# Rotated keys in one stacked tile, read once; queries' high and low parts held in both halves

## The chip, the cores and the metric

The kernel runs on one core of one Trainium2 chip. The metric is the device time of one execution in microseconds, lower is better. Of the kernel before there are three timed runs, and one more execution that was taken with a profile.

## What is computed

One layer of a bidirectional encoder for two sequences, a prompt of 512 tokens and a sample of 256, both 2048 wide, with shared weights. The kernel treats them as one block of 768 columns (`T`). Cut to what matters here:

```python
h = rmsnorm(x, ln_mix_g); z = h @ w_in         # [fourier 1024 | q 1024 | k 256 | v 256]
q, k = apply_rope(q, cos, sin), apply_rope(k, cos, sin)
s = einsum('bnqhgd,bnkhd->bnhgqk', qb, kb) * HEAD_DIM ** -0.5   # 16 q heads, 4 kv heads, width 64
p = exp(s - m) / (sum(exp(s - m)) + exp(sink - m))              # window of +-128 positions
mixed = concat([rmsnorm(of), rmsnorm(p @ v)])
x = x + mixed @ w_out
u = relu(rmsnorm(x) @ w_up); x = x + (u * u) @ w_down           # 2048 -> 8192 -> 2048
return rmsnorm(x, ln_final_g)
```

## The kernel before

All matrix products are made at nearly full float32 precision: an operand is split into a high part (rounded to the type that TensorE multiplies, `F32R`) and a low part (what is left), and three products, high by high, high by low and low by high, are added up in PSUM. Scores are an exception with a trick, described below.

**Stages.** The program runs through four stretches on one TensorE queue, whose order is written out by hand:

1. Norm of x, v projection, and the Fourier columns of `w_in` (in the profile up to 173.5 us).
2. Twenty pieces of q and k columns of `w_in` (five pairs of 128-column blocks, four pieces each; the products are `pz`, L802), with the Fourier transform between them, and the rotation of keys and queries beside them on the other engines (173.5 to 379 us).
3. Attention, 24 units (six blocks of 128 queries times four kv heads), interleaved with the first half of the output projection `pm` (L1046; 379 to 589 us). A unit is four heads. The order of this stretch is set by a list of events at due times (`t_qk`, `t_lq` and the like), counted in slots of the output projection.
4. The rest of the output projection, `w_up` (`pu`, L1193) and `w_down` (`pd`, L1628), to the end.

**Rotation and split (`cross`, `turned`, `parts`).** Columns come out of TensorE into PSUM and are copied by ScalarE to a tile `zs` of 128 partitions, two blocks and 768 columns (L815). Pair 0 holds the keys; it and pair 1 are parked in DRAM first and loaded back by `load_z`. GpSimd and VectorE rotate `zs` in place, ScalarE writes the high part to `zh`, VectorE writes the low part over `zs`, and ScalarE's DMA queue puts both into DRAM (L704): `kh`, `kl` for keys, `qh0` to `qh3` and `ql0` to `ql3` for queries. The tile `zs` has one buffer in the pool `kp` and one in the pool `zo`; pairs 0, 1 and 4 use the first in turn, pairs 2 and 3 the second. So pair 3 can be copied out of PSUM only when pair 2 has been put into DRAM.

**Scores (`qk`, L848).** A head is 64 wide, so one unit's query tile `qs` holds the high part in partitions 0 to 63 and the low part in 64 to 127. The keys stand in two tiles of 128 partitions: `kdh` has the high part in both halves, `kdl` the low part in both. Two products per head give (high + low) by low and (high + low) by high:

```python
def load_k(i):                                                        # L717
    h = slice(i % 2 * HD, (i % 2 + 1) * HD)
    nc.sync.dma_start(f32(kt["kdh" if i < 2 else "kdl"][h]), kr_d[i // 2][:].rearrange("(d h) t -> d h t", h=NKV))
...
qs = kt["kp"].tile([P, 4, P], F32R, tag="qs", name="qs", bufs=2)      # L727, in load_q
for o in range(2):
    nc.sync.dma_start(f32(qs[o * HD : (o + 1) * HD]), qr_d[g][o][:, t0].rearrange("(d h) t -> d h t", h=4))
...
for i in range(4):                                                    # L755
    after(14.5 + i, lambda i=i: load_k(i))
```

`load_k` (L719) makes four loads of 768 KB into 64 partitions each. `load_q` (L730) makes two loads of 128 KB per unit, into the two halves of one of two `qs` buffers; unit u + 2 is asked for when unit u's scores are done, since it takes unit u's buffer. Until the first units, the same two buffers serve as `zh`.

**Queues.** SP issues the loads: weights (`raw`, L79 and L162), Fourier outputs (`ofr`, L188), attention outputs (`oar`, L965), keys and queries. ScalarE's queue issues the puts: `kh` to `ql3`, attention outputs `oad` (L940) and projection results `y1` (L1079). Each queue issues in the order of its program, and an issue that waits holds back everything behind it. DMAs of both queues take eight completion semaphores in turn, and an issue also waits until the DMA that had its semaphore before, eight back over both queues, has landed. SP's order is written by a scheduler up to piece 18, and by hand from piece 19 through attention.

Of the kernel before, what the change touches and what calls it, by code (L numbers as in the profile page):

```python
# [11 lines left out]
F32 = mybir.dt.float32  # L12
F32R = mybir.dt.float32r
# [7 lines left out]
P = 128  # L21
# [3 lines left out]
T = SEQ + DSEQ  # L25
# [6 lines left out]
NKV = 4  # L32
HD = 64
# [7 lines left out]
def hybrid_encoder(ctx: ExitStack, tc: tile.TileContext, a: dict):  # L41
    nc = tc.nc
    ctx.enter_context(tc.manual_schedule(engines={mybir.EngineType.PE}))

    def f32(ap):
        return ap.bitcast(F32)
# [3 lines left out]
    dpool = ctx.enter_context(tc.tile_pool(name="dpool", bufs=1, space=DRAM))  # L50
# [63 lines left out]

    zf_d = [dpool.tile([P, T], F32, tag=f"zf{i}", name=f"zf{i}") for i in range(FG)]
    zs_d = [dpool.tile([2 * P, T], F32, tag=f"zs{i}", name=f"zs{i}") for i in range(2)]
    kr_d = [dpool.tile([2 * P, T], F32, tag=f"k{c}", name=f"k{c}") for c in "hl"]
    qr_d = [[dpool.tile([2 * P, T], F32, tag=f"q{c}{i}", name=f"q{c}{i}") for c in "hl"] for i in range(NKV)]
    of_d = dpool.tile([FG * P, T], F32, tag="of", name="ofd")
    oa_d = [dpool.tile([NH * HD, P], F32, tag=f"oa{i}", name=f"oad{i}") for i in range(NM)]  # L120
# [77 lines left out]
    with ExitStack() as ph:  # L198
# [454 lines left out]
        zo = {}  # L653

        kt = {}

        def open_attention():
            kp = kt["kp"] = kctx.enter_context(tc.tile_pool(name="kp", bufs=1, side="right", reuse_waits="tile"))
            for name, shape, src in (
                ("mask", [P, 384], a["c_mask"]), ("cosr", [P, T], a["c_cos"]), ("sinr", [P, T], a["c_sin"]),  # L660
                ("sink", [P, 64], a["attn_sink"].partition_broadcast(P)),
            ):
                kt[name] = kp.tile(shape, F32, tag=name, name=name)
                nc.sync.dma_start(kt[name][:, : src.shape[1]], src)
            for t in (kt["cosr"][:], kt["sinr"][:]):
                nc.vector.tensor_tensor(out=t, in0=t, in1=rb[:], op=ALU.mult)
            for name in ("kdh", "kdl"):
                kt[name] = kp.tile([P, NKV, T], F32R, tag=name, name=name)

        zt = {}  # L670
        t_zl, t_zp = 1.1, 1.9

        def z_tile(pair):
            zt[pair] = (zo["p"] if pair in (2, 3) else kt["kp"]).tile([P, 2, T], F32, tag="zs", name="zs")

        def load_z(pair):
            z_tile(pair)
            nc.sync.dma_start(zt[pair][:], zs_d[pair][:].rearrange("(b p) t -> p b t", p=P))
# [10 lines left out]
        def turned(pair, s):  # L689

            ts = slice(s * 256, (s + 1) * 256)
            z, y = zt[pair][:, :, ts], ys.pop((pair, s))
            cb = kt["cosr"][:, ts].rearrange("p (o t) -> p o t", o=1).to_broadcast([P, 2, 256])
            nc.vector.tensor_tensor(out=z, in0=z, in1=cb, op=ALU.mult)
            for b, op in enumerate((ALU.subtract, ALU.add)):
                nc.vector.tensor_tensor(out=z[:, b], in0=z[:, b], in1=y[:, b], op=op)  # L696

        def parts(pair, s, when=lambda dt, fn: fn()):

            ts = slice(s * 256, (s + 1) * 256)  # L700
            z = zt[pair][:, :, ts]
            out, scale = (kr_d, None) if pair == 0 else (qr_d[order[pair]], HD ** -0.5)
            hi = kt["kp"].tile([P, 2, 256], F32R, tag="zy" if pair == len(cols) - 1 else "qs", name="zh", bufs=2)
            put = lambda o, x: nc.scalar.dma_start(out[o][:, ts].rearrange("(b p) t -> p b t", p=P), x)  # L704
            if scale is None:
                nc.scalar.activation(hi[:], z, AF.Copy)
                low = lambda: nc.vector.tensor_tensor(out=z.bitcast(F32R), in0=z, in1=f32(hi[:]), op=ALU.subtract)
            else:
                nc.scalar.activation(hi[:], z, AF.Copy, scale=scale)
                low = lambda: nc.vector.scalar_tensor_tensor(  # L710
                    out=z.bitcast(F32R), in0=z, scalar=scale, in1=f32(hi[:]), op0=ALU.mult, op1=ALU.subtract
                )
            put(0, f32(hi[:]))
            when(t_zl, low)
            when(t_zp, lambda: put(1, z))

        def load_k(i):  # L717
            h = slice(i % 2 * HD, (i % 2 + 1) * HD)
            nc.sync.dma_start(f32(kt["kdh" if i < 2 else "kdl"][h]), kr_d[i // 2][:].rearrange("(d h) t -> d h t", h=NKV))  # L719

        units = [(b, g) for b in range(NM) for g in range(NKV)]
        state = {}
# [1 line left out]
        def load_q(u):  # L724
            b, g = units[u]
            t0 = slice(b * P, (b + 1) * P)
            qs = kt["kp"].tile([P, 4, P], F32R, tag="qs", name="qs", bufs=2)  # L727
            state[u] = {"qs": qs}
            for o in range(2):
                nc.sync.dma_start(f32(qs[o * HD : (o + 1) * HD]), qr_d[g][o][:, t0].rearrange("(d h) t -> d h t", h=4))  # L730

        todo = {}

        def after(piece, fn):
            todo.setdefault(piece, []).append(fn)

        for g in range(FG):
# [6 lines left out]
            after(p0 + 2, lambda g=g: stage2(g))  # L744
        after(10, fourier_norm)
        after(10, open_attention)
        cols = [2048, 1536, 1024, 1280, 1792]
        order = [None, 2, 0, 1, 3]
        for pair, t, ahead in ((0, 10.5, 10), (2, 11.5, None), (3, 15, None), (1, 16.5, 12)):
            if ahead is not None:  # L750
                after(ahead, lambda pair=pair: load_z(pair))
            for s in range(3):
                after(t + s // 2 * 0.5, lambda pair=pair, s=s: cross(pair, s))
                after(t + 0.5 + s // 2 * 0.5, lambda pair=pair, s=s: (turned(pair, s), parts(pair, s)))
        for i in range(4):  # L755
            after(14.5 + i, lambda i=i: load_k(i))
        for u in range(2):
            after(18 + 0.5 * u, lambda u=u: load_q(u))
        after(18, lambda: load_of(0, [kt["kp"].tile([P, 4, P], F32, tag="zy", name="ofr", bufs=2) for _ in range(2)]))
# [28 lines left out]
        for piece in range(n_in):  # L788
            pair, j = divmod(piece, 4)
# [6 lines left out]
            for c in range(2):  # L796
                cs = slice(c * P, (c + 1) * P)
                for i in range(4):
                    first, stop = j == 0 and i == 0, j == 3 and i == 3
                    for w, o, n in ((wh, 0, 0), (wh, 1, 1), (wl, 0, 2)):  # L800
                        for s in range(2):
                            nc.tensor.matmul(  # L802
                                ps[c][s][:, :HALF], w[:, i, cs], whole[j // 2][s][o][:, 4 * (j % 2) + i, :],
                                start=first and n == 0, stop=stop and n == 2,
                            )
                if j == 3:
                    if c == 0 and pair >= 2:
                        z_tile(pair)
                    if pair < 2:
                        zs = fp.tile([P, T], F32, tag="zs", name="zs", bufs=2)  # L810
# [19 lines left out]
    att = ExitStack()  # L830
    ap_ = att.enter_context(tc.tile_pool(name="att", bufs=2, reuse_waits="tile"))
    pp3 = att.enter_context(tc.tile_pool(name="pp3", bufs=1, space=PSUM, reuse_waits="tile"))
    mask, sink, kdh, kdl = (kt[c] for c in ("mask", "sink", "kdh", "kdl"))

    def key_blocks(b):
        lo, hi = (0, 3) if b < 4 else (4, 5)
        return max(lo, b - 1), min(hi, b + 1)

    def qk(u, heads):
        b, g = units[u]  # L840
        k0, k1 = key_blocks(b)
        nk = (k1 - k0 + 1) * P
        st = state[u]
        for h in heads:
            s = tiles.pop("s", None) or pp3.tile([P, 512], F32, tag="s", name="s", bufs=3)
            st[f"s{h}"] = s
            for n, kd in enumerate((kdl, kdh)):
                nc.tensor.matmul(s[:, :nk], st["qs"][:, h, :], kd[:, g, k0 * P : k0 * P + nk], start=(n == 0), stop=(n == 1))  # L848

    def row_max(u, heads):  # L850
        b, g = units[u]
# [152 lines left out]
    for u in range(len(units)):  # L1004
        t = pace * u + t_first
        for h in range(4):
            dt = t_qk + d_qk * h
            at(t + dt, lambda u=u, h=h: qk(u, (h,)))
            at(t + dt + t_max, lambda u=u, h=h: row_max(u, (h,)))
            at(t + dt + t_exp, lambda u=u, h=h: exps(u, (h,)))  # L1010
        at(t + t_norm, lambda u=u: normalize(u))
        if u + 2 < len(units):
            at(t + t_lq + 2 * (u == 1), lambda u=u: load_q(u + 2))
        for kb in range(3):
            at(t + t_trans + d_trans * kb, lambda u=u, kb=kb: trans(u, kb))
            at(t + t_pv + d_pv * kb, lambda u=u, kb=kb: pv(u, kb))
    for s in range(3):
        at(t_cross[s], lambda s=s: cross(len(cols) - 1, s))
        at(t_turn[s], lambda s=s: turned(len(cols) - 1, s))
        at(t_parts[s], lambda s=s: parts(len(cols) - 1, s, later))  # L1020
# [472 lines left out]
    order = (4, 2, 6, 0, 1, 3, 5)  # L1493
# [62 lines left out]
    def put(m, q, gained, queue=nc.sync):  # L1556
        y = acc4(m, q)
        if gained:
            nc.scalar.activation(y, y, AF.Copy, scale=ry[:, m : m + 1])
        else:  # L1560
            nc.vector.scalar_tensor_tensor(
                out=y, in0=y, scalar=ry[:, m : m + 1], in1=ep["gf"][:, q * 512 : (q + 1) * 512], op0=ALU.mult, op1=ALU.mult
            )
        queue.dma_start(out_rows(m)[:, q * 512 : (q + 1) * 512], y)
# [73 lines left out]
    left_terms = {1: (a21_d, s_d[3])}  # L1638
    HP = NFF // 4
    kept, parts, ep = {}, {}, {}  # L1640

    dunits = [(kh, i, j) for kh in range(2) for i in order for j in range(HP // 2)]
# [169 lines left out]
```

## Time and profile before

| | |
|---|---|
| time, median of 3 runs | 2589.92 us (2589.88 to 2593.62) |
| the profiled execution's own time | 2589.64 us |
| its span in the profile | 2587.8 us |
| granted TensorE clock | 0.999 |
| busy TensorE, VectorE, ScalarE, GpSimd | 100%, 70%, 43%, 10% of the span |
| moved by DMA | 489.55 MB, 189 GB/s on average |

How to read it: a row of the timeline or of a group names engine, line, operation, the tile written and the tiles read. PE is TensorE's matmul, PEld its weight load, DVE is VectorE, ACT is ScalarE, POOL is GpSimd; SPq and ACTq are the DMA queues of SP and ScalarE. "Idle before" is idle time of that engine just ahead of the row, and the name behind the arrow is what ended it. The time to landing of a DMA runs from its issue until its completion semaphore is full.

### The profile page before, as it was taken

The numbers are of one execution on the slowest core, as the hardware profiler recorded it, in microseconds if no ns is written. First come the engines' busy times: TensorE is split into PE (matmuls) and PEld (weight loads), VectorE is DVE, ScalarE is ACT, GpSimd is POOL, SyncE is SP. The second block draws the span as 40 slices with busy tenths as digits, with TensorE's granted clock in tenths as the row PEclk, the third lists the DMA queues.
The fourth block names the chain that finished last, engine by engine and source line by source line (L and its number), as shares of the span: only waits on it lengthen the run. The fifth ranks groups of instructions, "written<-read, shape, count | busy, mean of one in ns | idle before, by whom it ended". The sixth has DMA issues, their size and how long they took to land.

```text
span 2587.8 us, 34953 instructions
## 1 busy us (share of the span) xinstructions
PE 2575.5 (100%) x13580; PEld 2358.4 (91%) x13580; DVE 1812.4 (70%) x2222; ACT 1124.0 (43%) x1574; POOL 249.6 (10%) x353
## 2 busy tenths in 40 slices
PE   9999999999999999999999999999999999999998
PEld 9999998888899999999999999988888888888887
DVE  7966568776555656555877877667776765777687
ACT  6545437674333333333444554433333333333335
POOL 1001332232201011000000000110000000000000
PEclk9999999999999999999999999999999999999999
DMA  7963385345664445456666666775543662555364
GB/s 255 309 223 113 126 237 185 115 138 192 220 197 156 162 161 187 160 189 240 212 213 232 230 215 208 245 304 178 181 155 112 219 234 82 179 179 164 99 207 155
DMA packets 268999, 489.55 MB, mean 189 GB/s; under 512 B 19568, under 2 KB 164000, under 8 KB 267424
## 3 DMA queue, kind: packets, MB, share of 16 engines
q1 hardware_dynamic: 197328, 321.26, 39.0%
q10 hardware_dynamic: 58688, 115.18, 11.8%
q0 software_dynamic: 12816, 50.87, 5.8%
q8 instruction: 107, 1.75, 0.3%
q14 instruction: 60, 0.49, 0.1%
HBM read 360.35 MB, written 126.88 MB: 188 GB/s over the span
## 4 chain that ended last, share of the span: by engine, by line
PE 94%; DVE 2%; DMA 1%; POOL 1%; ACT 0%; issue 0%; SPq 0%; ACTq 0%; POOLq 0%; DVEq 0%
PE pu L1193 36%; PE pd L1628 35%; PE pm L1046 9%; PE p L268 5%; PE pz L802 4%; PE pv L391 1%; PE o L924 1%; PE s L848 1%; PE t L905 1%; POOL zy L687 1%; DMA raw<-in_w_in 1%; PE ptx L137 0%; DVE zs L696 0%; PE pa L609 0%; PE pe L630 0%
## 5 line engine op out<-in xcount | busy, mean ns | idle before, releaser
L1193 PE MATMUL pu<-xf,wh 128*128 128x384 f32 x3072 | 780.8, 335 | 0.0
L1193 PEld LDWEIGHTS pu<-xf,wh 128*128 128x128 f32 x3072 | 554.2, 188 | 1.5 <-ACT o L1211 1.3
L1628 PE MATMUL pd<-wl,sh 128*128 128x512 f32 x1332 | 518.3, 389 | 0.0
L1628 PE MATMUL pd<-wh,sh 128*128 128x512 f32 x1332 | 518.3, 389 | 0.0
L1628 PE MATMUL pd<-wh,sl 128*128 128x512 f32 x1332 | 518.1, 389 | 0.0
L1193 PE MATMUL pu<-xf,wl 128*128 128x384 f32 x1536 | 513.7, 334 | 0.0
L1605 ACT ACTIVATE wh<-rd 128x1024 fp32r<-128x1024 f32 x200 | 202.4, 1054 | 522.2 <-PE pd L1628 416.9
L1615 DVE TENSOR_TENSOR wl<-rd,wh 128x1024 fp32r<-128x1024 f32 x200 | 236.2, 1222 | 226.1 <-ACT wh L1605 225.4
L1173 ACT ACTIVATE wh<-ur 128x1024 fp32r<-128x1024 f32 x160 | 170.0, 1063 | 382.5 <-PE pu L1193 201.8
L1628 PEld LDWEIGHTS pd<-wh,sl 128*128 128x128 f32 x1332 | 250.1, 188 | 52.0 <-DVE sl L1616 0.3
L1628 PEld LDWEIGHTS pd<-wh,sh 128*128 128x128 f32 x1332 | 250.2, 188 | 51.5
L1628 PEld LDWEIGHTS pd<-wl,sh 128*128 128x128 f32 x1332 | 250.2, 188 | 51.5
L1193 PEld LDWEIGHTS pu<-xf,wl 128*128 128x128 f32 x1536 | 288.6, 188 | 0.0
L1179 DVE TENSOR_TENSOR wl<-ur,wh 128x1024 fp32r<-128x1024 f32 x160 | 195.6, 1222 | 76.0 <-ACT wh L1173 76.0
L1214 DVE TENSOR_TENSOR o<-pu,o 128x768 f32<-128x768 f32 x160 | 152.9, 956 | 122.4 <-PE pu L1193 114.8
L1598 DVE TENSOR_TENSOR rd<-rd 128x1024 f32<-128x1024 f32 x112 | 131.8, 1219 | 0.0
L1193 PE MATMUL pu<-xs,wh 128*128 128x384 f32 x512 | 130.0, 334 | 0.0
L1173 ACT ACTIVATE wh<-sx 128x1024 fp32r<-128x1024 f32 x64 | 67.8, 1061 | 130.5 <-PE pu L1193 105.0
L268 PE MATMUL p<-xs,wh 128*128 128x384 f32 x448 | 114.0, 335 | 0.0
L1616 DVE TENSOR_TENSOR sl<-sr,sh 128x768 fp32r<-128x768 f32 x111 | 105.7, 952 | 0.0
L1179 DVE TENSOR_TENSOR wl<-sx,wh 128x1024 fp32r<-128x1024 f32 x64 | 78.2, 1223 | 23.8 <-ACT wh L1173 23.6
L1193 PEld LDWEIGHTS pu<-xs,wh 128*128 128x128 f32 x512 | 92.5, 188 | 0.0
(279 smaller groups left out, 3914.6 us busy)
## 6 DMA issues: line engine op xcount, KB each, us to landing
rd<-in_w_down SPq DMA_DIRECT2D x176, 512.0 KB, 5.2
ur<-in_w_up SPq DMA_DIRECT2D x128, 512.0 KB, 4.0
sr<-sd SPq DMA_DIRECT2D x95, 384.0 KB, 5.4
pd<-o ACTq DMA_DIRECT2D x60, 384.0 KB, 2.3
o<-pd POOLq DMA_DIRECT2D x60, 384.0 KB, 5.9
sd<-sm ACTq DMA_DIRECT2D x60, 384.0 KB, 2.7
raw<-in_w_in SPq DMA_DIRECT2D x38, 512.0 KB, 5.9
raw<-in_w_out SPq DMA_DIRECT2D x32, 512.0 KB, 4.2
```

Of the source, the lines that this page charges most:

```text
L268: nc.tensor.matmul(ps7[bank, g, r][:, :HALF], l[:, i, r * P : (r + 1) * P], x[:, o, 4 * e + i, :], start=(opens and e == 0 and i == 0 and ...
L802: nc.tensor.matmul(ps[c][s][:, :HALF], w[:, i, cs], whole[j // 2][s][o][:, 4 * (j % 2) + i, :], start=first and n == 0, stop=stop and n == 2,)
L1046: nc.tensor.matmul(ps, l(k), w[:, k % 2, :], start=(k == 0 and n == 0), stop=(k == 7 and n == 2))
L1173: nc.scalar.activation(wh[:], raw[:], AF.Copy)
L1179: nc.vector.tensor_tensor(out=wl[:], in0=raw[:], in1=f32(wh[:]), op=ALU.subtract)
L1193: nc.tensor.matmul(ps[:, t, :HALF], w[:, i, t * P : (t + 1) * P], xb[:, o, i, :], start=(s == first_of[bank] and i == 0 and n == 0), stop= ...
L1214: nc.vector.tensor_tensor(out=o, in0=src, in1=o, op=ALU.add)
L1598: add = lambda x, y, op: nc.vector.tensor_tensor(out=x[:], in0=x[:], in1=y[:], op=op)
L1605: nc.scalar.activation(wh[:], t[:], AF.Copy)
L1615: nc.vector.tensor_tensor(out=wl[:], in0=t[:], in1=f32(wh[:]), op=ALU.subtract)
L1616: nc.vector.tensor_tensor(out=sl[:], in0=sr[:], in1=f32(sh[:]), op=ALU.subtract)
L1628: nc.tensor.matmul(o, l[:, q, ts], w[:, ns], start=(j == j0 and (q, t) == (0, 0)), stop=(j == j1 and (q, t) == (1, 2)),)
```

## The change

High and low parts of the keys go to one DRAM tensor of 512 rows and are read by one load of 1536 KB into one tile `kd`: high part in partitions 0 to 63, low part in 64 to 127. Both products of a head now read `kd`; what differs is the query operand, whose tile holds the high part in both halves and the low part in both halves, and is loaded by four DMAs of 128 KB per unit in place of two. A unit's products are now low by (high + low) and high by (high + low), two per head as before and of the same sizes. The space that one key tile of 12 KB per partition leaves goes to the larger `qs` buffers and to a second `zs` buffer in `kp`; `zh` uses half of a `qs` buffer. The load of the keys is asked for once, after piece 15, in place of four times from piece 14.5 on.

```diff
-    kr_d = [dpool.tile([2 * P, T], F32, tag=f"k{c}", name=f"k{c}") for c in "hl"]
+    kr_d = dpool.tile([4 * P, T], F32, tag="k", name="k")
...
-            for name in ("kdh", "kdl"):
-                kt[name] = kp.tile([P, NKV, T], F32R, tag=name, name=name)
+            kt["kd"] = kp.tile([P, NKV, T], F32R, tag="kd", name="kd")
...
-            zt[pair] = (zo["p"] if pair in (2, 3) else kt["kp"]).tile([P, 2, T], F32, tag="zs", name="zs")
+            zt[pair] = zo["p"].tile([P, 2, T], F32, tag="zs", name="zs") if pair in (2, 3) else kt["kp"].tile([P, 2, T], F32, tag="zs", name="zs", bufs=2)
...
-            out, scale = (kr_d, None) if pair == 0 else (qr_d[order[pair]], HD ** -0.5)
-            hi = kt["kp"].tile([P, 2, 256], F32R, tag="zy" if pair == len(cols) - 1 else "qs", name="zh", bufs=2)
+            out, scale = ([kr_d[o * 2 * P : (o + 1) * 2 * P] for o in range(2)], None) if pair == 0 else (qr_d[order[pair]], HD ** -0.5)
+            if pair == len(cols) - 1:
+                hi = kt["kp"].tile([P, 2, 256], F32R, tag="zy", name="zh", bufs=2)
+            else:
+                hi = kt["kp"].tile([P, 2, 4, P], F32R, tag="qs", name="zh", bufs=2)[:, 0].rearrange("p (b h) t -> p b (h t)", b=2)
...
-        def load_k(i):
-            h = slice(i % 2 * HD, (i % 2 + 1) * HD)
-            nc.sync.dma_start(f32(kt["kdh" if i < 2 else "kdl"][h]), kr_d[i // 2][:].rearrange("(d h) t -> d h t", h=NKV))
+        def load_k():
+            nc.sync.dma_start(f32(kt["kd"][:]), kr_d[:].rearrange("(p h) t -> p h t", h=NKV))
...
-            qs = kt["kp"].tile([P, 4, P], F32R, tag="qs", name="qs", bufs=2)
+            qs = kt["kp"].tile([P, 2, 4, P], F32R, tag="qs", name="qs", bufs=2)
             state[u] = {"qs": qs}
-            for o in range(2):
-                nc.sync.dma_start(f32(qs[o * HD : (o + 1) * HD]), qr_d[g][o][:, t0].rearrange("(d h) t -> d h t", h=4))
+            for i in range(2):
+                for o in range(2):
+                    nc.sync.dma_start(f32(qs[i * HD : (i + 1) * HD, o]), qr_d[g][o][:, t0].rearrange("(d h) t -> d h t", h=4))
...
-        for i in range(4):
-            after(14.5 + i, lambda i=i: load_k(i))
+        after(15, load_k)
...
-            for n, kd in enumerate((kdl, kdh)):
-                nc.tensor.matmul(s[:, :nk], st["qs"][:, h, :], kd[:, g, k0 * P : k0 * P + nk], start=(n == 0), stop=(n == 1))
+            for o in range(2):
+                nc.tensor.matmul(s[:, :nk], st["qs"][:, 1 - o, h, :], kd[:, g, k0 * P : k0 * P + nk], start=(o == 0), stop=(o == 1))
```

SP's order around the keys, where `raw` is the next weight piece and `zs<-zs` the load of a parked pair (the number names its DRAM tensor). Before:

```order
L678 DMA zs<-zs_78 128x2x768
L79 DMA raw<-in_w_in 128x4x256 x2
L719 DMA kdh<-kh 64x3072
L678 DMA zs<-zs_79 128x2x768
L79 DMA raw<-in_w_in 128x4x256
L719 DMA kdh<-kh 64x3072
L79 DMA raw<-in_w_in 128x4x256
L719 DMA kdl<-kl 64x3072
L79 DMA raw<-in_w_out 128x2x512
L719 DMA kdl<-kl 64x3072
L79 DMA raw<-in_w_out 128x2x512
```

And now:

```order
L677 DMA zs<-zs_78 128x2x768
L79 DMA raw<-in_w_in 128x4x256
L677 DMA zs<-zs_79 128x2x768
L79 DMA raw<-in_w_in 128x4x256
L720 DMA kd<-k 128x3072
L79 DMA raw<-in_w_in 128x4x256 x2
L79 DMA raw<-in_w_out 128x2x512 x2
```

Three loads are gone from among the weight loads, the parked pair 1 is loaded two places earlier, and the one load of keys stands where the first of the four stood.

SP's order at attention units 3 and 4, where `qh_88` is the high part of head group 3, `qh_82` that of group 0, and `ofr` and `raw` are loads for the output projection. Before:

```order
L730 DMA qs<-qh_88 64x4x128
L730 DMA qs<-ql_89 64x4x128
L188 DMA ofr<-ofd 128x8x128 x2
L79 DMA raw<-in_w_out 128x2x512
L730 DMA qs<-qh_82 64x4x128
L730 DMA qs<-ql_83 64x4x128
L79 DMA raw<-in_w_out 128x2x512
```

And now, with the same groups under the numbers 87, 88 and 81, 82:

```order
L732 DMA qs<-qh_87 64x4x128
L732 DMA qs<-ql_88 64x4x128
L732 DMA qs<-qh_87 64x4x128
L732 DMA qs<-ql_88 64x4x128
L188 DMA ofr<-ofd 128x8x128 x2
L79 DMA raw<-in_w_out 128x2x512
L732 DMA qs<-qh_81 64x4x128
L732 DMA qs<-ql_82 64x4x128
L732 DMA qs<-qh_81 64x4x128
L732 DMA qs<-ql_82 64x4x128
L79 DMA raw<-in_w_out 128x2x512
```

Each unit has two more loads, and what stood behind the pair stands behind four. On TensorE, VectorE, ScalarE and GpSimd the order of instructions is the same as before; only the names of the key tiles differ.

More of the change, by code (lines that the diff above doesn't have):

```diff
@@ L832, in hybrid_encoder @@
     pp3 = att.enter_context(tc.tile_pool(name="pp3", bufs=1, space=PSUM, reuse_waits="tile"))
-    mask, sink, kdh, kdl = (kt[c] for c in ("mask", "sink", "kdh", "kdl"))
+    mask, sink, kd = (kt[c] for c in ("mask", "sink", "kd"))
     def key_blocks(b):
```

## The prediction

> **What bounds the kernel now.** I read the page first, then a table of stages around the change, then who makes TensorE wait in them. The page: TensorE is busy for the whole span, and the chain that ended last runs through it.
>
> ```profile
> span 2587.8 us, 34953 instructions
> PE 2575.5 (100%) x13580; PEld 2358.4 (91%) x13580; DVE 1812.4 (70%) x2222; ACT 1124.0 (43%) x1574; POOL 249.6 (10%) x353
> PE 94%; DVE 2%; DMA 1%; POOL 1%; ACT 0%; issue 0%; SPq 0%; ACTq 0%; POOLq 0%; DVEq 0%
> ```
>
> So an edit to loads can change the time only through TensorE's idle time, by closing a gap or opening one. The table of stages (window, its length, then busy time of each engine) shows how much idle time there is where the change acts: rotation of the keys and queries from 300 to 380, attention from 380 to 580.
>
> ```profile
> 300.00:380.00 80.00, 79.58 (x461) 78.73 (x460) 48.57 (x63) 28.79 (x35) 27.08 (x26) 1.00 0.74 223
> 380.00:580.00 200.00, 199.83 (x1053) 169.12 (x1052) 159.07 (x493) 142.89 (x352) 55.69 (x93) 1.00 0.48 147
> ```
>
> TensorE idles 80 - 79.58 = 0.42 us in the first and 0.17 us in the second. The list of waits for TensorE in 300 to 580 has one entry, and the timeline shows where it is: at the start of piece 16, for ScalarE's copy of pair 3 out of PSUM, with two waits of the weight loads beside it.
>
> ```profile
> PE pz L802 <- ACT zs L815: 0.4, 1, 0.4
> 345.33 0.19 PEld L802 LDWEIGHTS pz<-xf,wh 128*128 128x128 f32 x1 [0.74 <-ACT zs L815]
> 345.33 0.82 PE L802 MATMUL pz<-xf,wh 128*128 128x384 f32 x2 [0.42 <-ACT zs L815]
> 345.71 0.19 PEld L802 LDWEIGHTS pz<-xf,wh 128*128 128x128 f32 x1 [0.20 <-ACT zs L815]
> ```
>
> The chain of waits between 330 and 350 says why the copy was late: pair 3 takes the `zs` buffer of pair 2, whose last put needed 8.93 us to land. Earlier puts of the same size, from a stretch without key loads, needed 2.2 us (list of DMA issues, 316 to 323; last number is the median time to landing).
>
> ```profile
> 335.81 8.93 DMA ql<-zs
> 344.80 0.49 ACT zs L815
> kh<-zh ACTq DMA_DIRECT2D x3, 256.0 KB, 2.2
> ```
>
> **The change part by part.**
>
> *Scores.* As many products, of the same shapes. The groups of the two key tiles cost the same, 301 ns each, so which tile is read changes nothing: 0.
>
> ```profile
> L848 PE MATMUL s<-kdl,qs 128*128 128x256 f32 (+1 forms) x96 | 28.9, 301 | 0.0
> L848 PE MATMUL s<-kdh,qs 128*128 128x256 f32 (+1 forms) x96 | 28.9, 301 | 0.0
> ```
>
> *Key loads.* Four loads of 768 KB become one of 1536 KB. All instructions of the key loads' line, with min, median and max of the time to landing:
>
> ```profile
> L719 SPq DMA_DIRECT2D kdh<-kh x2: 507/516/524, 325.0 to 334.7; - x2
> L719 SPq DMA_DIRECT2D kdl<-kl x2: 470/488/507, 341.1 to 345.2; - x2
> DMA to landing us min/median/max: 8.1/9.2/10.8
> ```
>
> The one load now waits for the low parts too, as the load of pair 1 does today; that is issued at 333.76 (SP's timeline), which is the latest for the key load:
>
> ```profile
> 333.76 0.37 SPq L678 DMA_DIRECT2D zs<-zs  x1
> ```
>
> It is not on TensorE's path: at twice the 10.8 us it is in by 333.8 + 21.6 = 355.4, and the first score product is at 378.93 (below). What counts is what it stands beside. Before, the second load from 334.7 and the third from 341.1 ran around the put of 335.81, with the load of pair 1 between them. Now these are gone from that stretch: pair 1 no longer waits for pair 0's buffer and is loaded early, and of the key loads one is left, which starts ahead of the put. The put of 335.81 then lands sooner. It needs to gain only about a microsecond, since with a landing of up to 7.9 us the copy would be done 1 us earlier and the gap gone: -0.42 us, and with the weight load's second wait of 0.20, **-0.6 us**. Bounds: 0, if the key load holds back the put as the others did; -0.9, if both weight-load waits (0.74 and 0.20) count in full. The waits show nothing that would be late next there. The row of 8.93 beside 2.2 us goes with a rule of the Trainium skill, "DMA: Bandwidth & Descriptors", section "Queues, rings and completion order": a DMA engine takes turns between queues packet by packet, so that a queue with short packets advances slowly beside one with long ones. By that rule alone the merged load, twice as long, could hold the puts of 329 to 336 instead, and the gain would be 0 and the sum +1.1 in place of +0.5.
>
> *Second `zs` buffer.* Pair 4's copy no longer waits for pair 1's puts. No TensorE wait hangs on it (the one entry above is pair 3's): 0. The cover is TensorE's products of the second block of the last piece. SP's issue of pair 1 moves ahead of one weight load and of the first key load, at half a microsecond of issue, with that weight load 19 us away: 0.
>
> *Query loads.* 48 loads of 128 KB become 96. Issue costs 0.5 to 0.6 us each on SP, and the loads land 2.5 us after issue at best, 6.6 at worst.
>
> ```profile
> L730 SPq DMA_DIRECT2D qs<-qh x24: 512/512/561, 374.0 to 561.0; - x24
> L730 SPq DMA_DIRECT2D qs<-ql x24: 512/603/688, 374.6 to 561.5; - x24
> DMA to landing us min/median/max: 2.5/3.3/6.6
> ```
>
> Call e the time by which the fourth load of a unit lands later than the second did. A unit loses what e exceeds its margin by. Most units have more margin than the three that follow, units 0, 4 and 21: SP's issues (timeline), the time from issue to landing in the list of issues, in the same order, and TensorE's first product of the unit.
>
> ```profile
> 373.98 0.56 SPq L730 DMA_DIRECT2D qs<-qh  x1
> 374.61 0.69 SPq L730 DMA_DIRECT2D qs<-ql  x1
> qs<-qh SPq DMA_DIRECT2D x1, 128.0 KB, 2.6
> 378.93 0.28 PE L848 MATMUL s<-kdl,qs 128*128 128x256 f32 x1
> ...
> 402.07 0.52 SPq L730 DMA_DIRECT2D qs<-qh  x1
> 402.63 0.61 SPq L730 DMA_DIRECT2D qs<-ql  x1
> qs<-qh SPq DMA_DIRECT2D x1, 128.0 KB, 6.0
> qs<-ql SPq DMA_DIRECT2D x1, 128.0 KB, 5.8
> 408.54 0.41 PE L848 MATMUL s<-kdl,qs 128*128 128x384 f32 x1
> ...
> 545.70 0.52 SPq L730 DMA_DIRECT2D qs<-qh  x1
> 546.27 0.60 SPq L730 DMA_DIRECT2D qs<-ql  x1
> qs<-qh SPq DMA_DIRECT2D x1, 128.0 KB, 6.6
> qs<-ql SPq DMA_DIRECT2D x1, 128.0 KB, 6.3
> 553.61 0.28 PE L848 MATMUL s<-kdl,qs 128*128 128x256 f32 x1
> ```
>
> Unit 4 is the tight one: its second load lands at 402.63 + 5.8 = 408.4, and the product starts at 408.54. Margin 0. It is late because SP was held until 401 by the second of the two `ofr` loads ahead of it. Unit 21: 546.27 + 6.3 = 552.6, margin 1.0. Unit 0: the second landing is not in the trace; at the first one's 2.6 us it is 377.2, margin 1.7.
>
> Now e. Two more issues come 2 x 0.6 = 1.2 us later. Where loads queue up behind weights (units 4 and 21) the pair landed 0.36 and 0.3 us apart (408.07 and 408.43; 552.3 and 552.57), so two more transfers there cost 2 x 0.3 = 0.6 once issue is ahead. Between 0.6 and 1.2 I take 1.0 for unit 4, nearer to the issue, since by the fourth issue at about 403.8 part of the queue ahead of it has drained: **+1.0**. Unit 21: e of 1.0 against a margin of 1.0, **+0.1**. Unit 0: e of 1.2 against 1.7, 0. For the range e is 0.6 at least. At most it is 2.2: 1.2 of issue, and 1.0 more for a put of ScalarE that slips between. That would cost 2.2 + 1.2 + 0.5 = 3.9 us.
>
> What is queued behind the added issues: `ofr`, `raw` and `oar` loads, each 1.2 us later. They are asked for a slot or more ahead, and only the last of `w_out` for the first slot is used soon, by ScalarE and VectorE at 380: hidden behind the first unit's scores, at most those 1.2 if not. The 45 added turns of the eight semaphores make some of ScalarE's puts wait for a query load, with exponentials behind them; ScalarE idles 200 - 142.89 = 57 us in attention, so a stall of a microsecond does not reach TensorE: 0.
>
> *Sum*: -0.6 + 1.0 + 0.1 = **+0.5 us**. On the profiled execution's 2589.64 that is 2590.1; the median is 0.28 above that execution, so 2589.92 + 0.5 = **2590.4**. No change of over 0.2% (5.2 us), which is about what a measurement of this kernel can tell from none.
>
> **The rivals.**
>
> *Everything hides.* The queries are early enough even at unit 4 (its four loads land as close together as the pair does now, while the loads ahead land a little sooner), and the gap at 345 closes: -0.9 to -0.6, 2589.0 to 2589.3. For it: idle time in 300 to 580 is 0.59 in all. Against it: unit 4 has no margin. For the same reason no closing of gaps here gives more than 0.2%: faster would have to come from outside the change.
>
> *Loads one after another (slower).* If a load of a tile finishes only after the one before has run its whole course, each added load costs at least the 2.6 us of unit 0's first, and e is 5.2. Units 4, 21 and 0 alone lose 5.2 + 4.2 + 3.5 = 12.9 us: 2602.8. It decides from 3e - 2.7 = 5.2 on, so at e = 2.6. For it: each buffer of `qs` is asked for only when the unit before last is done, and nothing runs ahead. Against it: the pairs that land 0.3 us apart. The Trainium skill bears on this in "SBUF — State Buffer", section "The DMA setup-cost knee": a transfer pays some 2 us that do not grow with its size, and the next section says that two transfers into the two halves of the partitions do not add up their rates. Four in place of two would by these be the wrong way; that the fixed part does not overlap is what the 0.3 us contradict.
>
> *The key load does not get out of the way.* It waits for six puts in place of three, runs into the queries' puts, and the gap stays: +1.1, 2591.0.
>
> **How the numbers follow.** Forecast 0.50; the gap stays 0.15; everything hides 0.18; e between 2.2 and 2.6, or ScalarE's waits reach TensorE, 0.06; one after another 0.08; faster by over 0.2% by a cause that I don't see 0.03. The first three and half of the fourth lie within 0.2%: 0.86; slower 0.11. The range goes from all hidden, 2589.92 - 0.9 = 2589.0, to e = 2.2 with the gap left, 2589.92 + 3.9 = 2593.8.
>
> **What would show it right or wrong.** In the profile after: no wait of `pz` for `zs` at piece 16; one key load, landing well before 378; at unit 4 TensorE idle for about 1 us ahead of its first product with a query load as releaser, at unit 21 next to none, and none at unit 0; query loads landing no more than 1.2 us later after the first issue than now. Waits for query loads at many units, or a busy time of the scores other than 2 x 28.9 us, would make the prediction wrong.

## The result, and the profile after

The changed kernel takes 2594.41 us (median of 21 runs, 2591.99 to 2598.55), the kernel before 2591.19 us beside it (21 runs, 2588.35 to 2594.26). The ratio is 1.0013, 95% interval 1.0007 to 1.0019: slower by 3.2 us (1.8 to 4.9), still within 0.2%. The forecast was +0.5 us. The measured median lies 0.6 us above the top of the range.

The profiled execution after took 2594.04 us. Its page (first two rows) and the table of stages (last two; window, length, busy time of PE, PEld, DVE, ACT, POOL, granted clock, DMA share, GB/s):

```profile
span 2592.2 us, 35020 instructions
PE 2575.6 (99%) x13580; PEld 2357.8 (91%) x13580; DVE 1814.3 (70%) x2222; ACT 1124.3 (43%) x1574; POOL 253.2 (10%) x353
300.00:380.00 80.00, 80.00 (x465) 79.58 (x465) 49.00 (x63) 29.39 (x35) 30.08 (x27) 1.00 0.65 205
380.00:580.00 200.00, 195.69 (x1029) 165.12 (x1028) 155.60 (x484) 140.34 (x345) 54.70 (x90) 1.00 0.59 174
```

TensorE's busy time is that of before (2575.5). Its idle time fell from 0.42 to 0.00 us in the rotation, where the gap was to close, and rose from 0.17 to 4.31 us in attention, where the added loads are; the DMA share there went from 0.48 to 0.59. The list of TensorE's waits from 300 to 600 (in us: total, number, longest) and the timeline of its score products at the three places, where the last brackets give the idle time before:

```profile
PE s L849 <- DVE os L937: 2.9, 1, 2.9
PE s L849 <- DMA qs<-ql: 0.7, 1, 0.7
PE s L849 <- DVE mx L864: 0.5, 1, 0.5
400.96 0.48 PE L849 MATMUL s<-kd,qs 128*128 128x256 f32 x2 [0.52 <-DVE mx L864]
411.73 0.58 PE L849 MATMUL s<-kd,qs 128*128 128x384 f32 x2 [2.93 <-DVE os L937]
557.68 0.49 PE L849 MATMUL s<-kd,qs 128*128 128x256 f32 x2 [0.73 <-DMA qs<-ql]
```

These are the first products of units 3, 4 and 21. Two are put down to VectorE, but all three wait for loads. SP's issues ahead of units 3 and 4 and of the last load of unit 21 (timeline), and from the list of issues the last load's time to landing, in the order unit 3, 4, 21:

```profile
396.75 0.60 SPq L732 DMA_DIRECT2D qs<-ql  x1
397.39 3.49 SPq L188 DMA_DIRECT2D ofr<-ofd  x2
400.93 0.58 SPq L79 DMA_DIRECT2D raw<-in_w_out  x1
401.62 0.92 SPq L732 DMA_DIRECT2D qs<-qh  x1
402.58 0.61 SPq L732 DMA_DIRECT2D qs<-ql  x1
403.24 0.95 SPq L732 DMA_DIRECT2D qs<-qh  x1
404.23 0.64 SPq L732 DMA_DIRECT2D qs<-ql  x1
...
550.96 1.46 SPq L732 DMA_DIRECT2D qs<-ql  x1
...
qs<-ql SPq DMA_DIRECT2D x1, 128.0 KB, 4.1
...
qs<-ql SPq DMA_DIRECT2D x1, 128.0 KB, 7.4
...
qs<-ql SPq DMA_DIRECT2D x1, 128.0 KB, 6.6
```

The last loads land at 400.8, 411.6 and 557.5, each about 0.1 us ahead of the product that waits. The VectorE instructions named on two of the waits end just ahead of the product by coincidence: in e_zero3 below, the same product of unit 4 starts at 410.40, while L937 there runs until 410.74. And e_ctrl below, with fewer loads, has none of the three waits.

Measured against the usual distance from start to start there (0.23 us), the three lose 0.69, 3.10 and 0.89 us, 4.7 in all. Below, "loses" always means this. In idle time the account is -0.4 us in the rotation, +4.1 in attention, +0.5 ahead of 300 and +0.2 behind 600, where nothing was changed: together the 4.4 us by which the span is longer.

### The profile page after: what moved, and what is told of

Its sections match the earlier page's. It is cut to its first block, busy times and chain, and to the rows that moved or that the text cites. A ratio compares the mean times of both kernels' runs of the same rounds, so it can differ in the third digit from the quotient of the medians.

```text
span 2592.2 us, 35020 instructions
## 1 busy us (share of the span) xinstructions
PE 2575.6 (99%) x13580; PEld 2357.8 (91%) x13580; DVE 1814.3 (70%) x2222; ACT 1124.3 (43%) x1574; POOL 253.2 (10%) x353
## 4 chain that ended last, share of the span: by engine, by line
PE 97%; DMA 1%; DVE 1%; ACT 0%; issue 0%; SPq 0%; DVEq 0%; POOLq 0%; POOL 0%; ACTq 0%
PE pu L1194 36%; PE pd L1629 35%; PE pm L1047 9%; PE pz L803 6%; PE p L268 5%; PE pv L391 1%; PE o L925 1%; PE s L849 1%; PE t L906 1%; PE ptx L137 0%; PE pa L609 0%; PE pe L630 0%; DMA raw<-in_w_in 0%; PE pt L137 0%; DMA qs<-ql 0%; DMA ofr<-ofd 0%
```

## The experiments

**What does the loss come from? (e_ctrl)** Two loads a unit with the bytes of before, all else as changed. Both products then read the same query tile, with high over low, so the result leaves out two of the four partial products.

```
-            for i in range(2):
-                for o in range(2):
-                    ... dma_start(qs[i * HD : (i + 1) * HD, o], qr_d[g][o] ...)
+            for c in range(2):      # two heads each, high over low
+                ... dma_start(qs[:, 0, 2 * c : 2 * c + 2], qr_d[g] ...)
```

> The changed kernel with only two query loads of 128 KB a unit (two heads each, over 128 partitions): both products use the tile with high over low, so two of the four partial products are counted twice and two are missing. Number and bytes of the query loads are those of before, no engine has more work, and key load, second zs buffer and scores are as changed. Theory: the loss is made by the 48 added loads alone. No wait of a first score product above 0.3 us at units 3, 4 and 21, gap at piece 16 closed, time before less 0.3 to 0.8 us. Rival (key load, zs buffer, turns): waits of 2 us or more stay, 1 to 4 us above before.

Measured: 2589.29 us against 2590.72 of before, ratio 0.9994 (0.9985 to 1.0003). No wait of TensorE is left in the list from 300 to 600, and the stages are:

```profile
300.00:380.00 80.00, 80.00 (x465) 79.45 (x465) 49.76 (x65) 29.10 (x35) 28.17 (x27) 1.00 0.62 204
380.00:580.00 200.00, 199.87 (x1053) 169.22 (x1052) 159.07 (x492) 143.76 (x354) 57.03 (x94) 1.00 0.47 146
```

Idle time is 0.00 and 0.13 us, and the span 2587.2, 0.6 below that of before. So the key load, the second buffer and the scores cost nothing that shows, the gap stays closed, and the whole loss is made by the 48 added loads. The rival is out.

**Two attempts at this control that brought costs of their own (e_half, e_zero).** The first took the products over 64 rows (`qs[:HD]`, `kd[:HD]`), the second set the half that isn't loaded to zero (`nc.gpsimd.memset(qs[HD:], 0.0)`).

> The changed kernel with the second half's two query loads of each unit left out (two loads of 128 KB a unit, as before) and the score products taken over partitions 0 to 63 alone, so that the keys' low parts do not enter the scores; all else as changed. Theory: the whole loss is made by the 48 added loads. Then TensorE's waits at units 3, 4 and 21 (0.69, 3.10 and 0.89 us in the profile after) go, unit 4 loses at most 0.3, the gap at piece 16 stays closed, and the time is that of before less 0.4 to 0.8 us. Rival: the loss comes with the merged key load, the second zs buffer or other turns of the semaphores; then 2 us or more of waits stay between 380 and 580 and the time is 1 to 4 us above before.

> The changed kernel with the two query loads into partitions 64 to 127 of each unit left out and that half set to zero by GpSimd, so that the products stay 128 rows long and the keys' low parts add nothing. Theory: the loss is made by the 48 added loads alone. No wait of a unit's first score product above 0.3 us between 380 and 600, the gap at piece 16 closed, time that of before less 0.3 to 0.8 us. Rival (key load, zs buffer or turns of the semaphores): 2 us of waits or more stay there, 1 to 4 us above before.

Measured: e_half 2625.42 us (ratio 1.0134, 1.0119 to 1.0150), with no wait in attention at all; what its products of 64 rows cost is in the last section. e_zero 2592.85 us (1.0006, 0.9997 to 1.0015). There the waits of units 3 and 21 are gone, but VectorE is slowed beside the memset (last section), its own waits reach TensorE, the `ofr` load that waits for VectorE goes out at 402.17 (400.52 in the changed kernel), and unit 4's loads behind it: unit 4 loses 0.8 us. Neither decides the question; e_ctrl does.

**Issues or bytes? (e_two, e_thin, e_eight)** As many bytes from half the issues, a quarter of the bytes from as many issues, and as many bytes from twice the issues.

```
e_two    + for o in range(2): ... dma_start(qs[:, o], qr_d[g] ...)              # 2 x 256 KB
e_thin   + ... dma_start(qs[i * HD : (i + 1) * HD, o, 0:1], ...)                # 4 x 32 KB
e_eight  + ... dma_start(qs[i * HD + d0 : i * HD + d0 + HD // 2, o], ...)       # 8 x 64 KB
```

> The changed kernel with a query tile's high and low parts in one DRAM tensor and two loads of 256 KB over 128 partitions a unit: as many bytes as changed, half the issues. The second load reads the same rows as the first, so two of the four partial products are counted twice and two are missing. Theory I (issue: 0.6 us on SP each, and a turn of the semaphores each): the waits fall to none at units 3 and 21 and to 0 to 1.3 us at unit 4; time before less 0.6 to plus 0.9. Theory B (bytes: 256 KB in packets of 512 B more through the DMA engines a unit): about 3 us at unit 4 and 0.9 at unit 21 as in the profile after, time 2.5 to 4 us above before.

> The changed kernel with four query loads a unit, of one head alone (32 KB each in place of 128): the products of all four heads use the queries of head 0. Issues and turns as changed, a quarter of the bytes, half of those before. Theory now (issue and bytes share unit 4's 3.1 us about evenly, units 3 and 21 are issue): unit 4 waits 0.8 to 1.6 us, unit 3 0.3 to 0.7, unit 21 0.3 to 0.9. Issue alone: as in the profile after, 3.1, 0.7 and 0.9. Bytes alone: no wait at any of them.

> The changed kernel with each of a unit's four query loads cut in two of 64 KB (32 partitions): as many bytes, twice the issues. Theory I (issue): 4 x 0.6 = 2.4 us more a unit, so unit 4 waits 5.5 us if its own issues count alone and 7.9 if unit 3's ahead of it count too, unit 21 3.3, unit 3 3.1, and units 0, 1 and 8 with 1.1 to 2.3 us of margin begin to wait: 9 to 16 us above the changed kernel. Theory B (bytes): waits as in the profile after, time within 1 us of the changed kernel.

Measured: e_two 2590.93 us (ratio 1.0001, 0.9992 to 1.0010), e_thin 2588.87 (0.9993, 0.9984 to 1.0002), e_eight 2605.30 (1.0054, 1.0040 to 1.0067). In e_two unit 4 loses 1.4 us and units 3 and 21 nothing, and TensorE waits 0.5 us for ScalarE's part of an `ofr` load. In e_thin unit 4 loses 0.3 and the others nothing. In e_eight unit 0 loses 1.4, unit 4 3.4, unit 8 0.5, unit 21 3.3 and unit 3 nothing, and TensorE waits 2.4 us for ScalarE's part of an `ofr` load that had fallen behind; three stretches at half the clock come on top (last section). Neither plain theory holds. Four issues without the bytes are nearly free, the bytes from two issues cost 1.4 of the 3.1 us, and only both together cost the whole; e_thin came out below what I expected of an even share. SP's timeline ahead of unit 4, of e_thin (first two rows) and of e_eight:

```profile
400.65 0.45 SPq L732 DMA_DIRECT2D qs<-qh  x1
...
402.43 0.59 SPq L732 DMA_DIRECT2D qs<-ql  x1
...
405.19 1.42 SPq L735 DMA_DIRECT2D qs<-qh  x2
406.65 1.56 SPq L735 DMA_DIRECT2D qs<-ql  x2
410.84 1.82 SPq L735 DMA_DIRECT2D qs<-qh  x2
413.45 1.18 SPq L735 DMA_DIRECT2D qs<-ql  x2
```

In e_thin the fourth issue is 1.8 us behind the first, in the changed kernel 2.6 (401.62 to 404.23). In e_eight SP stands 2.6 us between the fourth and the fifth: the fifth waits for the landing of the DMA eight before it in the turn of the semaphores, an `ofr` load. So with many bytes on the way an issue can have more to wait for; how much of unit 4's loss comes this way isn't shown.

**What stands ahead of unit 4's loads? (e_zero3, e_zero4)** As e_zero, for one unit only.

> As e_zero, but for unit 3 alone: all other units have their four loads. It tells what unit 4's 3.1 us are made of. If unit 3's two added loads push the ofr load ahead of unit 4's back and so count at unit 4 too: unit 3 waits 0, unit 4 waits 1.2 to 2.0 us. If only unit 4's own added loads count: unit 4 waits 3.0 to 3.8 us (unit 3's 0.7 comes on top). Unit 21 as in the profile after, 0.9, in both.

> As e_zero, but for unit 4 alone. If the wait at unit 4 is its own loads and what stands ahead of them in about equal parts: unit 3 waits 0.7, unit 4 1.2 to 2.0 us. If its own loads alone: 0 to 0.3. If what stands ahead alone: 2.8 or more. Unit 21 as in the profile after, 0.9.

Measured, one execution each (2593.61 and 2593.99 us). Unit 3 loses nothing in e_zero3; in e_zero4, whose DVE delays come on top, it has no wait for its loads. Unit 4 loses 2.0 us in e_zero3 and 0.95 in e_zero4. Unit 21 loses 1.7 and 2.0 where I expected 0.9, with the same instructions there as in the changed kernel; and unit 3, which loses 0.7 in the changed kernel, loses nothing with the same four loads in e_zero4, e_order and e_zs1. So a wait of this kind differs by up to a microsecond between executions. From unit 4's first issue to its last landing:

| kernel | loads of unit 3 / unit 4, KB | us |
|---|---|---|
| before | 2 x 128 / 2 x 128 | 402.07 to 408.4: 6.3 |
| e_ctrl | 2 x 128 / 2 x 128 | 400.70 to 407.0: 6.3 |
| e_zero | 2 x 128 / 2 x 128 | 403.27 to 410.2: 7.0 |
| e_thin | 4 x 32 / 4 x 32 | 400.65 to 407.1: 6.5 |
| e_zero4 | 4 x 128 / 2 x 128 | 402.87 to 410.0: 7.1 |
| e_two | 2 x 256 / 2 x 256 | 401.22 to 408.7: 7.5 |
| e_zero3 | 2 x 128 / 4 x 128 | 402.13 to 410.3: 8.1 |
| changed | 4 x 128 / 4 x 128 | 401.62 to 411.6: 10.0 |
| e_zs1 (below) | 4 x 128 / 4 x 128 | 401.57 to 411.9: 10.3 |

Against before, unit 4's own two added loads make 1.8 us (e_zero3), unit 3's 0.8 (e_zero4), both together 3.7. But e_zero, with none of them, takes 0.7 longer too. So the 0.8 isn't clear of what single executions differ by, and whether the two parts add up stays open.

**Is it the place in SP's queue? (e_order)** Unit 4's loads ahead of the second `ofr` load, unit 21's ahead of one weight load.

```
-            at(t + t_lq + 2 * (u == 1), lambda u=u: load_q(u + 2))
+            at(t + {1: 3.5, 2: -2.04, 19: 0.35}.get(u, t_lq), lambda u=u: load_q(u + 2))
```

> The changed kernel with unit 4's four query loads issued ahead of the second ofr load and of a weight load (after one ofr load instead of after two and a weight load), and unit 21's ahead of one weight load; nothing else moved. Theory (place in SP's queue): unit 4's loads are issued from about 398 instead of 401.6 and landed by 405, unit 21's 1.5 to 2 us earlier; the waits there (3.10 and 0.89) go, unit 3's 0.69 stays; the time is before plus 0.0 to 0.4 us, 3 us under the changed kernel. Rival (the loads' own length is what counts, or the transfers ahead do not shrink): unit 4 keeps 1 us or more, or another unit begins to wait by as much.

Measured: 2590.09 us against 2590.64, ratio 0.9997 (0.9988 to 1.0005). SP's timeline, to compare with the rows of the result:

```profile
397.12 0.62 SPq L188 DMA_DIRECT2D ofr<-ofd  x1
397.85 0.89 SPq L732 DMA_DIRECT2D qs<-qh  x1
400.18 0.61 SPq L732 DMA_DIRECT2D qs<-ql  x1
400.88 0.55 SPq L188 DMA_DIRECT2D ofr<-ofd  x1
```

Unit 4's loads land by 405.5, 7.7 us after the first issue in place of 10.0, and its first product starts at 407.78 without a wait; unit 21 has none either. So what stands ahead in the queue counts. Unit 3, where I expected its 0.69 us to stay, has none. What is late next shows at once: the `ofr` load now behind them reaches ScalarE 2.3 us late, VectorE's row maxima queue behind it, and unit 4's second product loses 0.5 us. Unit 8 loses 0.4.

**Both together (e_three_order).** A unit's queries in three loads (one of 256 KB with high over low, two of 128 KB with low over high; the same four partial products), in the order of e_order.

```
+            ... dma_start(qs[:, 0], qr_d[g] ...)                       # high over low
+            for o in range(2): ... dma_start(qs[(1 - o) * HD : (2 - o) * HD, 1], ...)
```

> The changed kernel with a query tile's high and low parts in one DRAM tensor, the first of the two products taken with high over low (one load of 256 KB over 128 partitions) and the second with low over high (two loads of 128 KB): the same four partial products from three loads a unit in place of four; and unit 4's and unit 21's loads issued earlier, as in e_order. Theory (issues and place in the queue): no wait of a first score product above 0.3 us at units 3, 4, 8 and 21; time before less 0.2 to 0.8 us. Rival (bytes decide): a wait of 0.4 us or more stays at unit 8 or comes at another unit, and the time is that of e_order within 0.5 us.

Measured: 2589.28 us (11 runs, 2588.66 to 2590.83) against 2590.27, ratio 0.9994 (0.9985 to 1.0003). The list of TensorE's waits from 300 to 600 is empty, and the span is 2587.0:

```profile
300.00:380.00 80.00, 80.00 (x466) 79.54 (x465) 49.41 (x64) 29.52 (x35) 28.57 (x27) 1.00 0.64 207
380.00:580.00 200.00, 199.86 (x1052) 169.09 (x1052) 159.42 (x493) 143.67 (x353) 56.84 (x94) 1.00 0.58 177
```

The DMA share is 0.58, as in the changed kernel, and nothing waits for it. The version keeps the whole change and recovers its loss. That it beats the kernel before, by 0.8 us of span, is not shown: the interval holds 1.

**Which part closed the gap at piece 16? (e_zs1)** One `zs` buffer beside the rotation (`bufs=2` taken out).

> The changed kernel with one zs buffer beside the rotation, as before, in place of two. The load of pair 1 then waits for pair 0's last put again. If the second buffer closed the gap at piece 16: the gap is back with 0.3 to 0.7 us of wait for ScalarE's copy. If the merged key load closed it by no longer running beside the put of pair 2: no gap, the put lands in under 8 us. The waits at units 3, 4 and 21 stay as in the profile after within 0.4 us each in either case.

Measured: 2594.99 us (ratio 1.0014, 1.0005 to 1.0023). The gap is not back (idle time from 300 to 380 is 0.00), so the second buffer isn't needed to close it. But that the key load closes it by staying out of the put's way is not what happens here: it runs from 331.14 to 339.64, beside the put. What differs is that the rotation starts earlier. SP's waits around 300, in the kernel before and in e_zs1, and ScalarE's last put of pair 2 and copy of pair 3 in e_zs1:

```profile
SPq L664 <- POOL ssf L641: 6.7, 1, 6.7
SPq L664 <- PE pz L630: 2.8, 1, 2.8
332.60 0.37 ACTq L706 DMA_DIRECT2D ql<-zs  x1
340.91 0.86 ACT L816 COPY zs<-pz 128x384 f32<-128x384 f32 x2 [2.47 <-PE pz L803]
```

L664 loads the constants; behind them SP issues the load of pair 0, at 303.48 before and at 299.57 here (299.0 to 300.5 in all kernels with the change). Before, the constants waited for GpSimd, now they wait for a TensorE product that is done sooner; the record doesn't show why, but the change laid out the pool anew in which these tiles stand. The last put of pair 2 so goes out 3.2 us earlier than the 335.81 of before, and even with the 8.93 us of before it would land at 341.5, well ahead of the 344.80 of the copy there. When it did land isn't in the record. Unit 4 loses 4.2 us and unit 21 1.5, more than the 0.4 I allowed, and unit 3 nothing, though the order of issues ahead of unit 4 is that of the changed kernel. One more thing shows there (last section).

## Why the prediction was wrong

- **Scores, 0:** right. The mean is 301 ns as before; the prediction's sign of 2 x 28.9 us of busy time was a bad one, since a group's busy time counts overlapping products once, and two groups have become one (42.3).

```profile
L849 PE MATMUL s<-kd,qs 128*128 128x256 f32 (+1 forms) x192 | 42.3, 301 | 4.2 <-DVE os L937 2.9 <-DMA qs<-ql 0.7 <-DVE mx L864 0.5
```

- **Key load and gap, -0.6:** right in sign and about in size (idle time -0.42; e_ctrl's span -0.6). The load goes out at 326.0 and lands in 8.1 us, at 334.1, ahead of the put that mattered. That put goes out at 336.12 and the copy starts at 341.07, so it landed in at most 4.9 us in place of 8.93. The earlier start of the rotation, which e_zs1 shows closing the gap as well, was not in the prediction. The puts beside the load were slow (8.6 and 9.1 us at the median in the list of issues, 2.2 before in a free stretch). They held ScalarE's next split back by 7.85 us, so the last put went out no earlier than before, but no copy waited for them. The rule that the prediction cites from the Trainium skill, "DMA: Bandwidth & Descriptors", section "Queues, rings and completion order", on queues taking turns, speaks of these puts; whether turns or a plain sharing of the DMA engines made them slow isn't shown.

```profile
kd<-k SPq DMA_DIRECT2D x1, 1536.0 KB, 8.1
qh<-zh ACTq DMA_DIRECT2D x2, 256.0 KB, 8.6
ql<-zs ACTq DMA_DIRECT2D x2, 256.0 KB, 9.1
```

- **Second buffer, 0, and unit 0, 0:** right.
- **Unit 4, +1.0: the step that failed.** Measured +3.1. The margin of 0 was right, the term e was mis-sized. As the prediction defines it, e was 3.2 us: the fourth load lands at 411.6, the second one of before at 408.4. That is above the bounds of 0.6 to 2.2. Of it, 1.5 is the fourth load behind the second of the same unit, within the bounds. The other 1.7 was put at nothing without a reason: the sum took the second load's landing as fixed, and it came at 410.1 though the unit's first issue was 0.45 us earlier than before (8.5 us after that issue in place of 6.3). Why it came later is shown in part. What stands ahead counts: with one `ofr` load in place of two and a weight load between the units (e_order), all four were in 7.7 us after the first issue, not 10.0. How much unit 3's added loads and unit 4's own do to it can't be told apart: with only one of the two sets the second load came after 7.1 (e_zero4) and 7.2 us (e_zero3), with neither after 6.3 (e_ctrl) to 7.0 (e_zero). Unit 3's stand in the same queue ahead of `ofr` and weights, so that "what is queued behind the added issues", priced at 0 because `ofr` is asked for early, was at the same time what is queued ahead of the next unit's queries.
- **Unit 21, +0.1:** measured +0.9 here and 1.5 to 2.0 in three other profiles. The fourth load landed 8.6 us after the unit's first issue, the second of before after 6.9, so e was 1.7 in place of 1.0; the fourth issue took 1.46 us on SP, not 0.6.
- **Unit 3, not priced:** +0.7. It was among the units with room because its first load landed 6.3 us ahead. Its second had no landing in the trace of before, but SP's timeline had its issue, 3.7 us after SP was done with the first, held until a put landed. At 2.5 us at best it lands at 398.4, so the margin to the product (last row) was 2.4 at most. And in the changed kernel the fourth load landed 2.6 us behind the second (400.83 and 398.18).

```profile
391.67 0.51 SPq L730 DMA_DIRECT2D qs<-qh  x1
395.89 0.51 SPq L730 DMA_DIRECT2D qs<-ql  x1
400.75 0.29 PE L848 MATMUL s<-kdl,qs 128*128 128x256 f32 x1
```

- **ScalarE's puts behind query loads, 0:** nothing in the runs speaks against it.
- **Rivals.** "Everything hides" describes e_ctrl and e_three_order, not the change. "One after another" (e of 5.2) is out: the four landed 0.4 to 1.0 us apart. The range ended at e = 2.2 for unit 4, which was 3.2.

The median of before was 2591.19 in the session of the result, 1.3 us above the one that the prediction started from; so of the 4.0 us by which it missed, 2.7 were the change's own.

## What to carry to other kernels

Price added transfers by the whole queue, not by the unit: list what stands ahead of each tight transfer and ask what the same edit did to that, too. A margin is only as good as the last landing it is read from; where the trace has none, take the issue and the best landing. When a load is late, look at its place in the issuing queue first: here moving two units' loads ahead in the queue took away most of the loss, and three loads in place of four the rest, with no byte less. And when a gap closes as forecast, check in the trace that it closed for the reason forecast: here a second reason would have sufficed.

## What the runs showed of the hardware that was not expected

**A wait can halve the clock, and where it falls decides.** Stretches of 3.41 us of e_eight (first two rows), of e_zs1 (next two) and of the changed kernel (last two); the first time behind the length is TensorE's busy time, the column ahead of the DMA share is the granted clock:

```profile
386.25:389.67 3.42, 0.98 (x6) 0.68 (x5) 1.24 (x6) 1.22 (x2) 0.00 (x0) 1.00 1.10 321
389.67:393.08 3.41, 3.41 (x10) 2.73 (x11) 3.34 (x9) 2.15 (x8) 0.00 (x0) 0.50 0.45 122
...
408.38:411.79 3.41, 0.00 (x0) 0.00 (x0) 2.05 (x5) 1.78 (x4) 0.00 (x0) 1.00 0.58 194
411.79:415.20 3.41, 3.16 (x10) 2.80 (x11) 2.69 (x12) 2.72 (x8) 0.00 (x0) 0.50 1.04 278
...
407.20:410.61 3.41, 1.60 (x10) 0.99 (x8) 2.41 (x8) 1.99 (x6) 0.00 (x0) 1.00 1.01 274
410.61:414.03 3.42, 2.30 (x13) 2.04 (x14) 2.38 (x8) 2.17 (x6) 0.00 (x0) 1.00 0.67 206
```

In e_eight the wait of 2.4 us for `ofr` halved the clock, in the changed kernel the wait of 2.9 us did not. So the length alone does not decide. The clock changes only in steps of 3.41 us: the three stretches at 0.50 in e_eight start at 389.67, 416.98 and 567.16, which are 8 and 44 such steps apart. The 2.4 us lay within one step, which left 0.98 us of busy time in it; the 2.9 us lay across two, with 1.60 and 2.30 us busy. Counted in these steps from the clock's first rise, every step of the 13 traces with TensorE busy for up to 1.54 us was followed by one at 0.50, and none with 1.56 us or more was. In a step at half clock the products lose another 1.5 (e_zs1) to 1.6 us (e_eight, units 4 and 21).

The Trainium skill, "TensorE: Matmul & The Clock Gate", Part 1, gives a free-running idle window of about 3.4 us, after which the clock is halved, and as long a busy one until it is back. Its length and its running free of the waits agree; that the window has to be idle throughout does not, with 0.98 us of products in the one of e_eight. By these numbers (an estimate) a wait of under 1.8 us does not halve the clock in a busy stretch, and one of 3.8 always does.

Ten of the 21 runs of the changed kernel show a mean clock of 0.998 (median 2595.41 us), the others, the profiled one among them, 0.999 (2593.64). The profile of e_zs1, with one step at half clock, also shows 0.998. So probably many of these runs had such a step, and it is part of their 3.2 us; without traces of them that is not shown.

**Products over half the rows break the overlap.** In e_half the 96 pairs of 64-row products cost 34.8 us over before, 0.36 us a pair, though they have no more columns. Groups of e_half, where the changed kernel has 301 for the scores and 418 for the second group:

```profile
L849 PE MATMUL s<-kd,qs 64*128 64x256 f32 (+1 forms) x192 | 51.7, 349 | 0.0
L1047 PE MATMUL pm<-wh,ofh 128*128 128x512 f32 x192 | 87.3, 454 | 0.0
```

In the timeline the weight load of a 64-row product starts only with the product (397.42 and 397.43), in the changed kernel 0.22 us ahead of it (403.81 and 404.03). From start to start, the steps to, across and behind such a pair are 0.33, 0.43 and 0.33 us there, and 0.22, 0.23 and 0.24 in the changed kernel.

**GpSimd's memset slows VectorE.** Timeline of unit 0's normalization in the changed kernel, and in e_zero with the memset beside it:

```profile
390.18 1.14 DVE L894 TENSOR_SCALAR p<-p,rs 128x256 f32<-128x256 f32 x4
...
390.28 1.92 DVE L897 TENSOR_SCALAR p<-p,rs 128x256 f32<-128x256 f32 x4
390.47 1.06 POOL L735 MEMSET qs<- 64x1024 f32 x1 [4.51 <-PE s L852]
```

0.78 us more for the four instructions, beside a memset of 1.06 us. In e_zero3 and e_zero4, with one memset each (at 390.55 and 398.29), TensorE's one wait for VectorE of over 0.2 us between 386 and 402 comes right behind it (0.44 us at 391.90, 0.49 at 400.05).
